# Up and gate products of a gated MLP by Strassen's scheme over even and odd tokens

## The chip, the core and the metric

The kernel runs on one core of one Trainium2 chip. The metric is the device time of one execution in microseconds (us), the median of the runs shown. A separate profiled execution gives the trace; its time is given beside the runs.

## The reference, cut to what matters

One decoder block over 1024 tokens with 16 meta tokens ahead of them, all in float32. The mixer (short convolution and stick-breaking attention) comes first; its output projection, a norm and a residual follow; then the gated MLP, which is the part that the change rewrites:

```python
D_MODEL, SEQ, N_META, CONV_WIDTH, D_FF = 1024, 1024, 16, 3, 2816

def conv_gated_mlp(xn, w_up_gate, conv_w_ffn, w_down):
    u, g = jnp.split(xn @ w_up_gate, 2, axis=-1)     # each (tokens, 2816)
    u = causal_dwconv(u, conv_w_ffn)                 # 3 taps per channel, along tokens
    return (jax.nn.gelu(u) * g) @ w_down

h = h + rms_norm(mix, g_post_mix)
h = h + rms_norm(conv_gated_mlp(rms_norm(h, g_pre_ffn), ...), g_post_ffn)
return h[:, N_META:, :]
```

## The kernel before

Every float32 product is made of three matmuls: an operand is split into a rounded part `hi` (a cast on ACT) and the remainder `lo` (a subtraction on POOL or DVE, in `split`), and hi x hi, hi x lo and lo x hi are added up in PSUM. 1026 tokens count for the MLP (1024 and two before them for the convolution), in three chunks of 342 or nine blocks of 114.

The stage before the MLP is the out-projection: for each of nine token blocks, `out_chunk` makes three PSUM chunks (24 matmuls each), and `post_block` does the first norm, the residual, and the second norm on DVE and ACT, ending in the row `xv`. A block's transposes (`transposed`, on PE) are emitted one block later; before, they write the MLP's input `xn2` straight from PSUM as hi and lo.

The MLP has 22 channel blocks of 128 for u and 22 for the gate. Each is an item of the class `Dense`: 512 KB of weights come in one DMA on the SP queue, are split once, and three chunks of 24 matmuls (8 feature blocks x 3) follow. A step of the outer loop (`NG` = 11) makes two u items and two gate items. Copies of u go to SBUF on ACT; `conv3` and the gelu run on ACT and DVE; a gate chunk is multiplied from PSUM on DVE, and the product is split into `ahi` and `alo`, the stationary operands of the down product. Down weights are split on POOL. A step's down product (`down`: 8 token blocks x 2 halves, 512 columns) is handed out between the dense chunks of the next step; the last step takes four channel blocks at once, and a norm, the residual and the output DMA follow per token block.

Engines take their instructions in order; a scheduler in the build orders them per engine from the written program and its dependencies. Tiles of a pool share buffers, and the first writer of a new tile waits for the last user of the old one.

Of the kernel before, what the change touches and what calls it, by code (L numbers as in the profile page):

```python
# [26 lines left out]
EPS = 1e-6  # L27


@with_exitstack  # L30
def block_kernel(ctx, tc, x, meta_tokens, g_pre_mix, w_in, channels, w_proj_conv,
# [28 lines left out]
    mm_d = tc.dram_tile([7, P, KB * QB], F32, name="mm_d")  # L60
    h_d = tc.dram_tile([NQ, D], F32, name="h_d")
# [94 lines left out]
    def col_block(w, c):  # L156
        return w[c]
# [407 lines left out]
    xnt_ctx.close()  # L565
    slots_de = ctx.enter_context(ExitStack())
# [3 lines left out]
    m_ctx = ctx.enter_context(ExitStack())  # L570
    mpool = m_ctx.enter_context(pool("mblk", 2))
# [54 lines left out]
    xn2 = []  # L626
    CHU = [(0, CH), (CH, CH), (2 * CH, CH)]
    CHG = [(2, CH - 2), (CH, CH), (2 * CH, CH)]
# [27 lines left out]
    s_ctx.close()  # L656
    psA.close()
# [6 lines left out]

    o_ctx = ctx.enter_context(ExitStack())
    ow = o_ctx.enter_context(pool("ow", 1, "right"))
    osml = o_ctx.enter_context(pool("osml", 4, "right"))
    g_post = ow.tile([P, D], F32, name="g_post")
    g_pre2 = ow.tile([P, D], F32, name="g_pre2")
# [3 lines left out]
    xn2 = [slot_tile(pl, "xn2") for pl in (slotD, slotE, slotF)]  # L673

    ff_items, act, conv_in = [], {}, {}
    dense3 = Dense(ps_mm2, ff_items)
# [3 lines left out]
    def load_m(b):  # L680
        if b in mb or b > 8:
            return
        raw = mpool.tile([P, KB, QB], F32, name="mraw", tag="mraw")
        nc.sync.dma_start(raw, mm_d[b - 2].rearrange("p (k n) -> p k n", k=KB))
        t = m_tile(b)
        split(t[:, 0], t[:, 1], raw)

    def out_chunk(b, c, ssq):
# [10 lines left out]
        sq = ow.tile([P, CH], F32, name="sq", tag="sq")  # L699
        nc.scalar.activation(sq[:QB, :n], ps, AF.Square, accum_out=ssq[:QB, c:c + 1])  # L700
        nc.vector.tensor_tensor(rows[b][:QB, cs], ps, g_post[:QB, cs], op=ALU.mult)

    def post_block(b, ssq):
        t = b * QB
        h = rows[b][:QB]
        xv = ow.tile([P, D], F32, name="xv", tag="xv", bufs=2)[:QB]
# [15 lines left out]
        def transposed():  # L722
            c, o = b // 3, (b % 3) * QB
            to_features(xn2[c][:, 0, :, o:o + QB], xn2[c][:, 1, :, o:o + QB], xv, QB, ps_tp2)
# [3 lines left out]
    ffn = {}  # L728

    def item_u(fb):  # L730
        def evac(ci, a, n, ps):
            if ci == 0:
                if fb == 0:
                    wk = slotC.tile([P, 2, KB, CH], F32, name="owork", tag="t")
                    ffn["wk"] = wk.rearrange("p a k n -> p (a k n)")
                conv_in[fb] = (ffn["wk"][:, fb * NQ:(fb + 1) * NQ] if fb < 2 else
                               ffn["u"].tile([P, NQ], F32, name="u", tag="u"))
            u = conv_in[fb]
            nc.scalar.copy(u[:, a:a + n], ps)
            if ci == 2:  # L740
                cv = ffn["u"].tile([P, D], F32, name="cv", tag="cv")
                conv3(cv, u, D, lambda k: w_ffn(k, fb))
                nc.scalar.activation(cv, cv, AF.Gelu_apprx_tanh)
                conv_in[fb] = cv
        return (col_block(w_up_gate, fb), src_of(xn2), CHU, evac)

    def item_g(fb):
        def evac(ci, a, n, ps):
            if ci == 0:
                act[fb] = (ffn["p"].tile([P, D], F32R, name="ahi", tag="ahi", bufs=4),  # L750
                           ffn["p"].tile([P, D], F32R, name="alo", tag="alo", bufs=4))
            ah, al = act[fb]
            c = slice(a - 2, a - 2 + n)
            cv = conv_in[fb][:, c]
            nc.vector.tensor_tensor(cv, cv, ps, op=ALU.mult)
            split(ah[:, c], al[:, c], cv)
        return (col_block(w_up_gate, NFF + fb), src_of(xn2), CHG, evac)

    NG = NFF // 2
    for gi in range(NG):  # L760
        ff_items += [item_u(2 * gi), item_u(2 * gi + 1), item_g(2 * gi), item_g(2 * gi + 1)]

    to_transpose = []
    for b in range(9):
        load_m(b + 1)
        rows[b] = ow.tile([P, D], F32, name="row", tag="row", bufs=2)
        sums = osml.tile([P, 3], F32, name="sums", tag="sums")
        for c in range(3):
            out_chunk(b, c, sums)
        if to_transpose:  # L770
            to_transpose.pop(0)()
        if b == 7:
            dense3.load(0)
            dense3.prep(0)
            dense3.load(1)
        post_block(b, sums)


    first = [dense3.run(0), dense3.run(1)]
    for g in (first[0], first[0], first[1], first[1]):  # L780
        for _ in range(8):
            next(g)
        if to_transpose:
            to_transpose.pop(0)()
    o_ctx.close()
    slots_abc.close()
    m_ctx.close()
    fu = ctx.enter_context(pool("fu", 2, "right"))
    fp = ctx.enter_context(pool("ffn", 2))
    fsml = ctx.enter_context(pool("fsml", 4))  # L790
    ffn["p"], ffn["u"] = fp, fu
    accs = [fp.tile([P, D], F32, name=f"acc{i}", bufs=1) for i in range(8)]

    def down_weights(fb, pl, tag, engine):
        raw = wpool.tile([P, D], F32, name="raw", tag="raw")
        nc.sync.dma_start(raw, w_down[fb * P:(fb + 1) * P, :])
        hi = pl.tile([P, D], F32R, name=tag + "hi", tag=tag + "hi")
        lo = pl.tile([P, D], F32R, name=tag + "lo", tag=tag + "lo")
        split(hi, lo, raw, engine)
        return hi, lo  # L800

    ssqs = {}

    def down(gi, wd):
        last = gi == NG - 2
        nj = len(wd)
        for tb in range(8):
            if last:
                ssqs[tb] = fsml.tile([P, 2], F32, name="fs", tag="fs")
            for hf in range(2):  # L810
                if last and hf:
                    ps = ps_mm2.tile([P, 512], F32, name="mm", tag="mm")
                else:
                    ps = ps_o.tile([P, 512], F32, name="po", tag="po")
                c = slice(hf * 512, (hf + 1) * 512)
                for j in range(nj):
                    ah, al = act[2 * gi + j]
                    hi, lo = wd[j]
                    th, tl = ah[:, tb * P:(tb + 1) * P], al[:, tb * P:(tb + 1) * P]
                    nc.tensor.matmul(ps, th, hi[:, c], start=(j == 0), stop=False)  # L820
                    nc.tensor.matmul(ps, tl, hi[:, c], start=False, stop=False)  # L821
                    nc.tensor.matmul(ps, th, lo[:, c], start=False, stop=(j == nj - 1))  # L822
# [5 lines left out]
                if last:  # L828
                    sq = fu.tile([P, NQ], F32, name="sq", tag="u")[:, :512]
# [3 lines left out]
            yield tb  # L833

    def ffn_steps(gi):
        if gi == 0:
            for g in first:
                for _ in range(9):
                    next(g, None)
                yield  # L840
            dense3.i = 2
        for _ in range(6 if gi == 0 else 12):
            dense3.chunk()
            yield

    pend, wd = None, []
    for gi in range(NG):
        for s, _ in enumerate(ffn_steps(gi)):
# [91 lines left out]
```

## Time and profile before

| | us |
|---|---|
| median of 3 runs | 2108.33 (2107.0 to 2110.51) |
| the profiled execution | 2109.53 |
| span of its trace, first to last instruction | 2107.8 |
| out-projection | 1245.70 to 1352.90 |
| MLP, to its last matmul | 1352.90 to 2095.97 |
| from there to the end | 11.83 |

The engines are PE (matmuls), PEld (its weight loads), DVE, ACT, POOL, and SP, which here only issues DMAs. Busy times come from the hardware profiler; the end of a matmul is modelled, so the duration shown is longer than the time that it takes in a stream, and the distance from one start to the next tells the latter. A mark such as [0.21 <-DVE xv L720] is idle time of the engine ahead of the instruction, and what ended it.

### The profile page before, as it was taken

The page shows a single profiled execution, that of the slowest core. Times are in us where ns is not written, and L with a number is a line of the kernel's source. Part 1 is how long each engine was busy: PE and PEld are TensorE (multiplying, and loading weights), DVE is VectorE, ACT ScalarE, POOL GpSimd, SP SyncE. Part 2 cuts the span into 40 slices and gives each one's busy share as a digit, 9 for nine tenths or more (in the row PEclk, how much of TensorE's full clock was granted, in tenths as well). Part 3 has the DMA queues.
Part 4 walks back from the last instruction along what each step waited for, and adds up shares of the span by engine and source line. Part 5 has one row for each costly group of instructions (what it writes and reads, how often), then busy time and mean ns, then how long its engine had stood idle before and what let it go on. Part 6 is the DMA issues. An engine that isn't in the chain of part 4 may idle for free.

```text
span 2107.8 us, 30776 instructions
## 1 busy us (share of the span) xinstructions
PE 2042.4 (97%) x12624; PEld 1958.1 (93%) x12624; DVE 1008.1 (48%) x1613; ACT 786.6 (37%) x1642; POOL 684.4 (32%) x591
## 2 busy tenths in 40 slices
PE   5999999999999999999999999999999999999997
PEld 5999999999999999999999999999999999999996
DVE  6455565655555555654331116543333343333436
ACT  4444454545454444544421124332222221222232
POOL 4443444444344434444122540032112221222123
PEclk9999999999999999999999999999999999999999
DMA  3111101111111111012584674221011110111124
GB/s 132 41 51 41 61 31 55 47 43 41 48 51 41 60 32 61 31 53 74 168 237 151 179 219 126 63 70 50 25 57 51 51 50 31 61 51 51 30 81 139
DMA packets 49689, 154.49 MB, mean 73 GB/s; under 512 B 12024, under 2 KB 12024, under 8 KB 49548
## 3 DMA queue, kind: packets, MB, share of 16 engines
q1 hardware_dynamic: 48396, 150.43, 22.7%
q8 instruction: 99, 1.62, 0.3%
q10 hardware_dynamic: 1152, 2.10, 0.3%
q14 instruction: 42, 0.34, 0.1%
HBM read 119.83 MB, written 32.68 MB: 72 GB/s over the span
## 4 chain that ended last, share of the span: by engine, by line
PE 86%; DVE 7%; ACT 3%; DMA 2%; issue 2%; POOL 1%; SPq 0%; DVEq 0%; ACTq 0%; POOLq 0%
PE mm L125 20%; PE mm L126 20%; PE mm L127 20%; PE po L820 3%; PE po L822 3%; PE po L821 3%; PE tp L369 3%; PE av L359 2%; PE av L360 2%; PE z L323 2%; PE z L322 2%; PE po L695 2%; PE po L697 2%; PE po L696 2%; DVE fl L333 1%
## 5 line engine op out<-in xcount | busy, mean ns | idle before, releaser
L66 POOL TENSOR_TENSOR wlo<-raw,whi 128x1024 fp32r<-128x1024 f32 x124 | 312.4, 2520 | 660.9 <-ACT whi L65 660.9
L125 PE MATMUL mm<-xnT,whi 128*128 128x342 f32 (+2 forms) x1536 | 508.3, 331 | 3.6 <-ACT xnT L65 3.6
L126 PE MATMUL mm<-xnT,whi 128*128 128x342 f32 (+2 forms) x1536 | 495.6, 323 | 0.5 <-DVE xnT L66 0.5
L127 PE MATMUL mm<-xnT,wlo 128*128 128x342 f32 (+2 forms) x1536 | 494.0, 322 | 0.0
L125 PE MATMUL mm<-xn,whi 128*128 128x342 f32 (+1 forms) x1056 | 337.8, 320 | 0.0
L126 PE MATMUL mm<-xn,whi 128*128 128x342 f32 (+1 forms) x1056 | 337.7, 320 | 0.0
L127 PE MATMUL mm<-xn,wlo 128*128 128x342 f32 (+1 forms) x1056 | 336.4, 319 | 0.0
L335 POOL TENSOR_TENSOR be<-be,fl 114x127 f32<-114x127 f32 (+2 forms) x144 | 176.9, 1228 | 404.0 <-DVE fl L333 193.2
L125 PEld LDWEIGHTS mm<-xnT,whi 128*128 128x128 f32 x1536 | 291.2, 190 | 8.3 <-ACT xnT L65 4.2
L126 PEld LDWEIGHTS mm<-xnT,whi 128*128 128x128 f32 x1536 | 292.0, 190 | 2.1 <-DVE xnT L66 1.0
L127 PEld LDWEIGHTS mm<-xnT,wlo 128*128 128x128 f32 x1536 | 291.2, 190 | 0.0
L65 ACT CAST whi<-raw 128x1024 fp32r<-128x1024 f32 x126 | 132.3, 1050 | 253.0 <-PE mm L126 221.2
L333 DVE TENSOR_TENSOR_SCAN fl<-fl 114x128 f32<-114x128 f32 (+2 forms) x144 | 204.9, 1423 | 4.9
L126 PEld LDWEIGHTS mm<-xn,whi 128*128 128x128 f32 x1056 | 199.7, 189 | 2.7
L125 PEld LDWEIGHTS mm<-xn,whi 128*128 128x128 f32 x1056 | 198.9, 188 | 2.8
L127 PEld LDWEIGHTS mm<-xn,wlo 128*128 128x128 f32 x1056 | 199.0, 188 | 0.0
L66 DVE TENSOR_TENSOR al<-tp,ah 128x342 fp32r<-128x342 f32 (+4 forms) x288 | 127.0, 450 | 139.5 <-ACT ah L65 137.5
L827 DVE TENSOR_TENSOR acc<-acc,po 128x512 f32<-128x512 f32 x136 | 93.1, 685 | 191.1 <-PE po L822 191.1
L65 ACT CAST ah<-tp 128x342 fp32r<-128x342 f32 (+4 forms) x288 | 112.9, 398 | 189.7 <-PE tp L369 181.8
L324 ACT ACTIVATE fl<-z 114x348 f32<-114x348 f32 (+10 forms) x240 | 111.4, 464 | 130.9 <-PE z L323 123.5
L369 PE MATMUL tp<-ident,be 114*128 114x114 f32 x720 | 119.6, 263 | 25.5 <-DVE al L66 20.9
L369 PEld LDWEIGHTS tp<-ident,be 114*128 114x128 f32 x720 | 89.1, 138 | 40.0 <-DVE al L66 29.7
(155 smaller groups left out, 3428.3 us busy)
## 6 DMA issues: line engine op xcount, KB each, us to landing
raw<-in_w_in_dram SPq DMA_DIRECT2D x64, 512.0 KB
raw<-in_w_up_gate_dram SPq DMA_DIRECT2D x44, 512.0 KB
raw<-in_w_down_dram SPq DMA_DIRECT2D x22, 512.0 KB
y_d<-yy SPq DMA_DIRECT2D x8, 513.0 KB
ga_d<-gt SPq DMA_DIRECT2D x8, 513.0 KB
o_d<-ot SPq DMA_DIRECT2D x8, 513.0 KB
gc_d<-gt SPq DMA_DIRECT2D x8, 513.0 KB
ld<-y_d SPq DMA_DIRECT2D x8, 513.0 KB
```

Of the source, the lines that this page charges most:

```text
L65: nc.scalar.copy(hi, src)
L66: (lo_engine or nc.vector).tensor_tensor(lo, src, hi.bitcast(F32), op=ALU.subtract)
L125: nc.tensor.matmul(ps, wh, xh, start=(kb == 0), stop=False)
L126: nc.tensor.matmul(ps, wh, xl, start=False, stop=False)
L127: nc.tensor.matmul(ps, wl, xh, start=False, stop=(kb == KB - 1))
L324: nc.scalar.activation(fl[:, c0:c0 + n], z, AF.Sigmoid, scale=-0.125)
L333: nc.vector.tensor_tensor_scan(fl[:, :nk][:, ::-1], fl[:, :nk][:, ::-1], fl[:, :nk][:, ::-1], 1.0, op0=ALU.mult, op1=ALU.min)
L335: nc.gpsimd.tensor_tensor(be[:, 0:nk - 1], be[:, 0:nk - 1], fl[:, 1:nk], op=ALU.mult)
L369: nc.tensor.transpose(tp[:n, QB * j:QB * (j + 1)], blocks[j][0][:, kb * P:kb * P + n], ident[:QB, :QB])
L820: nc.tensor.matmul(ps, th, hi[:, c], start=(j == 0), stop=False)
L821: nc.tensor.matmul(ps, tl, hi[:, c], start=False, stop=False)
L827: nc.vector.tensor_tensor(a, a, ps, op=ALU.add)
```

## The change

Up and gate products go by Strassen's scheme (Winograd's form), one level. The tokens are split into even (E) and odd (O), the 1024 features into two halves (1, 2), and two channel blocks of 128 make a pair; so each pair is a 2 x 2 by 2 x 2 product of blocks, with B11 = E1, B12 = O1, B21 = E2, B22 = O2 and weight quarters A11 to A22. Seven products of 12 matmuls take the place of eight. `x_early` and `x_late` make the seven token operands (B11, T1, T2, B21, T3, B22, T4) once, in two halves of 258 and 256 columns (`HALF`); `prep_pair` makes the seven weight operands of a pair with four sums on DVE, seven casts on ACT and seven subtractions on POOL, in a ring of eight tiles. A u pair runs two sets of products (258 and 256 columns), a gate pair one set of 512. `products` adds in PSUM: bank b1 is filled by A11 x B11, copied by ACT, and then gets S2 x T2 added, copied again, and so on. The out-projection's transposes now go to a float32 tile `xr`.

Down becomes a stage of its own: gated activations are stored to `act_d` in DRAM and loaded again, ten groups (nine of two channel blocks, one of four), with the same matmuls as before.

```diff
+HALF = [(0, 258), (258, 256)]
+NJ = 514
...
+    act_d = tc.dram_tile([DFF, D], F32, name="act_d")
...
-            to_features(xn2[c][:, 0, :, o:o + QB], xn2[c][:, 1, :, o:o + QB], xv, QB, ps_tp2)
...
+                        if j == 0:
+                            nc.scalar.copy(dst, src)
+                        else:
+                            nc.vector.tensor_copy(dst, src)
...
+    def x_early(c):
+        e1, o1 = quarter(c, "E1"), quarter(c, "O1")
+        op_split("B11", c, e1, nc.gpsimd)
+        sub(nc.vector, o1, o1, e1)
+        op_split("T1", c, o1, nc.vector)
+        sub(nc.vector, o1, quarter(c, "O2"), o1)
+        sub(nc.vector, e1, o1, e1)
+
+    def x_late(c):
+        op_split("T2", c, quarter(c, "O1"), nc.vector)
+        op_split("B21", c, quarter(c, "E2"), nc.gpsimd)
+        op_split("T3", c, quarter(c, "E1"), nc.vector)
+        sub(nc.vector, quarter(c, "E2"), quarter(c, "E2"), quarter(c, "O1"))
+        op_split("B22", c, quarter(c, "O2"), nc.gpsimd)
+        op_split("T4", c, quarter(c, "E2"), nc.vector)
...
+    def prep_pair(i):
...
+        keep("A11", a11)
+        nc.vector.tensor_tensor(tmp_s, a21, a22, op=ALU.add)
+        yield
+        keep("S1", tmp_s)
+        sub(nc.vector, a21, a11, a21)
+        sub(nc.vector, a11, tmp_s, a11)
+        yield
+        keep("S2", a11)
+        yield
+        keep("A12", a12)
+        sub(nc.vector, a12, a12, a11)
+        yield
+        keep("S3", a21)
+        yield
+        keep("S4", a12)
+        yield
+        keep("A22", a22)
+        load_pair(i + 1)
+        yield
...
+        b1, b3 = bank()[:, :n], bank()[:, :n]
+        mm(b1, "A11", "B11", True, True)
+        nc.scalar.copy(snap()[0][:, :n], b1)
+        yield
+        mm(b3, "S1", "T1", True, True)
+        nc.scalar.copy(snap()[1][:, :n], b3)
+        yield
+        mm(b1, "S2", "T2", False, True)
+        nc.scalar.copy(snap()[2][:, :n], b1)
+        yield
+        b2 = bank()[:, :n]
+        mm(b2, "A12", "B21", True, True)
+        evac(0, 0, b2, snap()[0][:, :n])
+        yield
+        mm(b1, "S3", "T3", False, True)
+        evac(1, 1, b1, snap()[1][:, :n])
+        yield
+        mm(b3, "S4", "B22", False, True)
+        evac(0, 1, b3, snap()[2][:, :n])
+        yield
+        mm(b1, "A22", "T4", False, True)
+        evac(1, 0, b1, None)
+        yield
...
+    def evac_g(p):
...
+            if s is None:
+                nc.vector.tensor_tensor(v, v, ps, op=ALU.mult)
+            else:
+                nc.vector.tensor_tensor(s, ps, s, op=ALU.add)
+                nc.gpsimd.tensor_tensor(v, v, s, op=ALU.mult)
...
+                nc.sync.dma_start(act_d[fb * P:(fb + 1) * P, :], cv)
...
+    for i in range(1, len(pairs)):
+        p, gate = divmod(i, 2)
+        if gate:
+            conv_gelu(p)
+            sets = [products(i, 1, 512, bank, evac_g(p))]
+        else:
+            sets = [products(i, j0, n, bank, evac_u(j0, n)) for j0, n in HALF]
...
+    groups = [[2 * g, 2 * g + 1] for g in range(9)] + [[18, 19, 20, 21]]
```

Two places where the order on an engine moves. The first is PE at the end of the out-projection: `po` is its last chunk, `tp_14167` (before) and `tp_14150` (after) are the transposes of the next-to-last token block, and `tp_14241` and `tp_14311` those of the last one, read from its `xv`. Before:

```order
L697 MATMUL po_14139<-w_o_12209,mb_13943 114x340
L175 MATMUL tp_14167<-ident_61,xv_14054 128x114 x4
L175 MATMUL tp_14174<-ident_61,xv_14054 128x114 x4
L125 MATMUL mm_14214<-xn2_13032,whi_14048 128x342
...
L126 MATMUL mm_14287<-xn2_13032,whi_14208 128x342
L175 MATMUL tp_14241<-ident_61,xv_14181 128x114 x4
L175 MATMUL tp_14248<-ident_61,xv_14181 128x114 x4
L127 MATMUL mm_14287<-xn2_13032,wlo_14209 128x342
```

After:

```order
L706 MATMUL po_14119<-w_o_12210,mb_13925 114x340
L735 MATMUL tp_14150<-ident_61,xv1_13048 128x114 x4
L735 MATMUL tp_14156<-ident_61,xv1_13048 128x114 x4
L844 MATMUL st_14215<-opB11_13038,a_op_14014 128x258
...
L848 MATMUL st_14216<-opT1_13039,a_op_14084 128x258
L735 MATMUL tp_14311<-ident_61,xv0_13047 128x114 x4
L735 MATMUL tp_14317<-ident_61,xv0_13047 128x114
L844 MATMUL st_14215<-opT2_14199,a_op_14116 128x258
```

Between the transposes of the last two blocks there stood 50 matmuls of 342 columns; now there stand 24 of 258, the first two products of the first pair.

The second is ACT from the end of a u pair to its gate pair. In the rows before, `u` are copies from PSUM, the ACTIVATE rows of `cv` the convolution's first tap and the gelu, `whi` the cast of a coming weight. Before:

```order
L65 CAST whi_15750<-raw_15632 128x1024
L739 COPY u_15659<-mm_15703 128x342
L193 ACTIVATE cv_15729<-u_15659,par_66 128x1024
L743 ACTIVATE cv_15729<-cv_15729 128x1024
L739 COPY u_15781<-mm_15756 128x342
```

After, with `a_op` a weight operand of the ring, `snap` the copy of a bank, `owork` the tile that holds u and cv:

```order
L68 CAST a_op_14740<-raw_14615 128x512
L859 COPY snap_14229<-st_14725 128x256
L68 CAST a_op_14770<-raw_14617 128x512
L68 CAST a_op_14800<-raw_14615 128x512
L68 CAST a_op_14829<-raw_14617 128x512
L196 ACTIVATE owork_14276<-owork_14276,par_66 128x1024
L897 COPY owork_14276<-st_14725 128x255
L196 ACTIVATE owork_14276<-owork_14276,par_66 128x1024
L68 CAST a_op_14859<-raw_14832 128x512
L853 COPY snap_14229<-st_14844 128x512
L976 ACTIVATE owork_14276<-owork_14276 128x1024
```

Where one cast of a whole weight stood, casts of half width stand between the bank copies, and the cast of the pair after next (`a_op_14859`, from the raw tile `raw_14832`) stands ahead of the gate pair's first bank copy (`st_14844`).

## Rows read from the trace of the kernel before

**Rows 1.** The page, part 1: engine, busy us (share of the span), instructions.

```profile
PE 2042.4 (97%) x12624; PEld 1958.1 (93%) x12624; DVE 1008.1 (48%) x1613; ACT 786.6 (37%) x1642; POOL 684.4 (32%) x591
```

**Rows 2.** Busy us (instructions): PE, PEld, DVE, ACT, POOL; granted clock, DMA share, GB/s.

```profile
1352.90:2095.97 743.07, 742.86 (x4241) 696.84 (x4239) 303.90 (x405) 187.77 (x287) 167.36 (x76) 1.00 0.17 56
2095.97:2107.80 11.83, 0.00 (x1) 0.00 (x0) 6.93 (x16) 1.65 (x5) 1.83 (x2) 0.62 0.24 89
```

**Rows 3.** Timeline of PE: start us, us, engine, line, operation; down, then gate.

```profile
1500.96 0.39 PE L820 MATMUL po<-dhi,ahi 128*128 128x512 f32 x1
...
1503.73 0.32 PE L125 MATMUL mm<-xn,whi 128*128 128x340 f32 x1
...
1505.92 0.32 PE L127 MATMUL mm<-xn,wlo 128*128 128x340 f32 x1
```

**Rows 4.** The page, part 5: operation, count, busy us, mean ns, idle.

```profile
L125 PE MATMUL mm<-xn,whi 128*128 128x342 f32 (+1 forms) x1056 | 337.8, 320 | 0.0
```

**Rows 5.** Timeline of PE: the two narrow kinds with full streams around them.

```profile
609.75 0.27 PE L359 MATMUL av<-ah,vv 128*128 128x228 f32 x1
609.86 0.27 PE L360 MATMUL av<-al,vv 128*128 128x228 f32 x1
609.97 0.33 PE L125 MATMUL mm<-xnT,whi 128*128 128x342 f32 x1
...
962.21 0.30 PE L322 MATMUL z<-kk,qh 128*114 128x292 f32 x1
962.34 0.29 PE L323 MATMUL z<-kk,ql 128*114 128x292 f32 x1
962.47 0.32 PE L125 MATMUL mm<-xnT,whi 128*128 128x342 f32 x1
```

**Rows 6.** Groups by line: casts and subtractions.

```profile
L66 POOL TENSOR_TENSOR wlo<-raw,whi 128x1024 fp32r<-128x1024 f32 x124 | 312.4, 2520 | 660.9 <-ACT whi L65 660.9
L65 ACT CAST whi<-raw 128x1024 fp32r<-128x1024 f32 x126 | 132.3, 1050 | 253.0 <-PE mm L126 221.2 <-DMA raw<-in_w_up_gate_dram 13.9 <-PE mm L127 6.2
L66 DVE TENSOR_TENSOR wlo<-raw,whi 128x1024 fp32r<-128x1024 f32 x2 | 2.5, 1226 | 0.9 <-ACT whi L65 0.9
L65 ACT CAST ahi<-cv 128x342 fp32r<-128x342 f32 (+1 forms) x66 | 31.2, 473 | 156.9 <-DVE cv L755 153.8 <-issue 3.0
```

**Rows 7.** Timelines of PE and ACT: a chunk's last matmul and its copy.

```profile
1369.67 0.31 PE L127 MATMUL mm<-xn,wlo 128*128 128x342 f32 x1
1370.03 0.45 ACT L739 COPY owork<-mm 128x342 f32<-128x342 f32 x1 [3.30 <-PE mm L127]
```

**Rows 8.** Timelines of SP and ACT: a weight load issued, its user.

```profile
1526.24 2.71 SPq L101 DMA_DIRECT2D raw<-in_w_up_gate_dram  x2
1529.90 1.05 ACT L65 CAST whi<-raw 128x1024 fp32r<-128x1024 f32 x1 [1.48 <-DMA raw<-in_w_up_gate_dram]
```

**Rows 9.** Timeline of PE: last matmul of the out-projection, transposes of the last block.

```profile
1352.67 0.33 PE L697 MATMUL po<-w_o,mb 128*114 128x340 f32 x1
...
1361.82 0.97 PE L175 MATMUL tp<-ident,xv 114*128 114x114 f32 x8 [0.21 <-DVE xv L720]
```

**Rows 10.** The columns of rows 2, around an idle stretch of PE.

```profile
968.00:972.00 4.00, 1.38 (x11) 1.10 (x10) 3.96 (x5) 0.95 (x3) 3.24 (x4) 1.00 0.51 130
972.00:976.00 4.00, 4.00 (x18) 4.00 (x18) 0.88 (x3) 0.69 (x2) 1.35 (x3) 0.57 0.00 0
976.00:980.00 4.00, 4.00 (x26) 3.91 (x25) 1.29 (x2) 2.29 (x6) 0.00 (x0) 1.00 0.00 0
```

**Rows 11.** Timelines of DVE and POOL where they work at the same time.

```profile
1378.60 3.30 POOL L66 TENSOR_TENSOR wlo<-raw,whi 128x1024 fp32r<-128x1024 f32 x1 [1.37 <-ACT whi L65]
1380.09 2.89 DVE L194 SCALAR_TENSOR_TENSOR cv<-owork,par,cv 128x1024 f32<-128x1024 f32 x1 [0.46 <-ACT cv L193]
1383.01 1.28 DVE L195 SCALAR_TENSOR_TENSOR cv<-owork,par,cv 128x1024 f32<-128x1024 f32 x1
```

**Rows 12.** The page, part 5: weight loads of up and gate.

```profile
L125 PEld LDWEIGHTS mm<-xn,whi 128*128 128x128 f32 x1056 | 198.9, 188 | 2.8
```

More of the change, by code (lines that the diff above doesn't have):

```diff
@@ L656, in block_kernel @@
     s_ctx.close()
+    slots_de.close()
     psA.close()
@@ L763, in block_kernel @@
     to_transpose = []
+    prep0 = prep_pair(0)
     for b in range(9):
         load_m(b + 1)
-        rows[b] = ow.tile([P, D], F32, name="row", tag="row", bufs=2)
+        rows[b] = rws[b % 2]
         sums = osml.tile([P, 3], F32, name="sums", tag="sums")
@@ L802, in block_kernel, with bank_of @@
[L802 to L806, printed above, removed]
+    ring_pool["ap"] = ctx.enter_context(pool("ap", 2, "right"))
+    late_ctx = ctx.enter_context(ExitStack())
+    late = late_ctx.enter_context(pool("late", 1, "right"))
+    for name in ("T2", "B21", "T3", "B22", "T4"):
+        ops[name] = late.tile([P, 2, 4, NJ], F32R, name=f"op{name}")
+    x_late(0)
+    def bank_of(pl, tag):
+        return lambda: pl.tile([P, 512], F32, name="st", tag=tag)
+    first = products(0, *HALF[0], bank_of(ps_mm2, "mm"), evac_u(*HALF[0]))
@@ new lines, in block_kernel @@
+    for k, _ in enumerate(first):
+        if k >= 1:
+            next(prep0, None)
+        if k == 5:
+            to_transpose.pop(0)()
+            x_early(1)
+            x_late(1)
+    for _ in prep0:
+        pass
+    prep = prep_pair(1)
+    for k, _ in enumerate(products(0, *HALF[1], bank_of(ps_o, "po"), evac_u(*HALF[1]))):
+        if k % 2:
+            next(prep, None)
+    psB.close()
+    psC = ctx.enter_context(ExitStack())
+    ps_st = psC.enter_context(pool("ps_st", 8, space=PSUM))
@@ new lines, in block_kernel @@
+    last_pair = len(pairs) - 1
+    for i in range(1, len(pairs)):
[3 more added lines that the diff above has]
+            sets = [products(i, 1, 512, bank, evac_g(p))]
+        else:
+            sets = [products(i, j0, n, bank, evac_u(j0, n)) for j0, n in HALF]
+        for _ in prep:
+            pass
+        prep = prep_pair(i + 1) if i < last_pair else prep_down_first()
+        for si, st in enumerate(sets):
+            for k, _ in enumerate(st):
+                if gate or (7 * si + k) % 2:
+                    next(prep, None)
@@ L807, in down @@
+    for gi, fbs in enumerate(groups):
+        last = gi == len(groups) - 1
+        for _ in prep:
+            pass
+        prep = iter(()) if last else prep_down(groups[gi + 1])
+        if gi == len(groups) - 2:
+            nc.sync.dma_start(g_post2, g_post_ffn.partition_broadcast(P))
+        if last:
+            for tb in range(2):
+                load_h(tb)
         for tb in range(8):
@@ L871, in block_kernel @@
[L871 to L882 removed]
+            next(prep, None)
```

318 lines of the change are left out of this document (192 added, 126 removed).

## Prediction

> **What bounds the kernel now.** I read the busy time first: TensorE (PE) works 97% of the span [rows 1]. Then the span in stages, the last one cut out: from the end of the out-projection (1352.90 us) to the last matmul PE is busy 742.86 of 743.07 us at a granted clock of 1.00, and 11.83 us of tail follow [rows 2]. DVE, ACT and POOL are busy 304, 188 and 167 us of those 743. So the change touches a stretch in which only matmuls set the time: whatever it takes from them is gained until another engine makes PE wait, and nothing hides such a wait.
>
> What a matmul costs is read from start to start, since the duration shown overlaps the next one. Twelve of 512 columns take 2.77 us, 0.231 each; fourteen of 340 take 2.19 us, 0.156 each [rows 3]. The stretch agrees: up and gate have 3 x 1056 = 3168 matmuls [rows 4], down has 22 x 16 x 3 = 1056 of 512 columns, 243.9 us; with about 1.2 us for the transposes of the last blocks, (743.07 - 243.9 - 1.2) / 3168 = 0.1572 us.
>
> **The products.** For each pair of channel blocks the old kernel issues 144 matmuls of 340 or 342 columns. The new one issues 84 per set: two sets (258 and 256 columns) for u, one of 512 for the gate. With 11 pairs of each kind that is 1848 narrow and 924 wide matmuls, 2772 in place of 3168. The wide ones cost 924 x 0.231 = 213.4 us. The trace has none of 258 columns. The nearest rows are 228 columns, with a full 128-column weight load, at 0.11 us, and 292 columns at 0.13 us [rows 5]; the line between them gives 0.119. I take 0.120 and keep 0.110 and 0.130 for the range: 1848 x 0.120 = 221.8 us (203 to 240). Before: 3168 x 0.1572 = 498.0. **Gain 62.8 us.** Down keeps its 1056 matmuls.
>
> By the Trainium skill, TensorE: Matmul & The Clock Gate, section Back-to-back issue gap, a warm matmul of N columns takes N/2.4 + 2.5 ns: 110 ns for 258 columns, and the sum would be 18 us lower. The trace differs: for 340 columns the rule gives 144 ns and the rows 156, so the rows stand.
>
> **Preparing the weights.** Per pair the old kernel made two casts (ACT, 1.05 us) and two subtractions (POOL, 2.52) of 1024 columns; the new one makes seven of 512 columns of each, plus four DVE sums. Half-width prices, between the shorter and the full rows [rows 6]: ACT 0.62, POOL 1.26, DVE 0.61 us. POOL gets 8.8 us per pair, 12.6 in a gate pair with three multiplications, ACT 4.3, DVE 2.5, against 20.2 us of PE for a u pair and 19.4 for a gate pair. In sum all fit; what counts is the order. The ring has eight operand tiles and a pair uses seven, so each new operand waits for the product one place earlier to finish, and six of the seven are made while the second set of u runs, one per product of 12 x 0.120 = 1.44 us. ACT is then in series with PE: the third product adds into the bank of the first, so it waits for the copy of that bank, and the order shows the operand's cast ahead of that copy. The hop from a product's last slot to ACT is 0.36 us after that matmul's start, 0.20 after its slot [rows 7]; 0.20 + 0.62 + 0.45 (the copy there, of 342 columns) = 1.27 us, against 1.44. It fits by 0.2.
>
> At the change from u to gate, ACT holds the cast of the pair after next ahead of the first bank copy. Its raw tile is freed by the S4 subtraction on POOL: not before 5 x 1.44 = 7.2 us into the second set, plus 0.20, 0.62 and 1.26, so 9.3, or 10.3 behind one busy DVE instruction. A 512 KB load took 3.66 us from issue to its user [rows 8]: it lands 2.9 to 3.9 us into the gate pair (the set ends at 10.1). Cast and copy bring it to 4.1 to 5.1; PE's third product is due at 2 x 2.77 = 5.5. Margin 0.4 to 1.4 us. In the other direction the gate pair's products are twice as long and nothing is close; its two stores of activations stand on SP's queue ahead of loads that wait for POOL longer than they do.
>
> With margins this thin I charge the 22 pairs 0.3 us each: **6 us**; ends 0 and 1.26 (one POOL instruction per pair, 28 us).
>
> **The start of the stage.** The last token block's row must pass norm, residual and second norm before its transposes: in the old kernel these started 9.0 us after the out-projection (1361.82 against 1352.67 and 0.16 for its last matmul), and PE filled that with 50 dense matmuls, waiting 0.21 us [rows 9]. The new order has 24 narrow matmuls there: 2.9 us and 0.75 of transposes, so PE stands still for about 5.3 us. What is late next is DVE: from 9.0 us on it stands in line with twelve operand instructions of 1.23 us, a copy and three evacuations (some 2 us), so the last operand of the second half is ready at 25.8; its 12 matmuls and about eight before them end at some 28. The pair's own PE work would have ended at 21.1. **Loss 7.** After an idle stretch the clock falls: 2.62 us of idle [rows 10] were followed by 4 us at a granted clock of 0.57, mostly the 1.2 GHz level, with 18 matmuls in place of 26, some 1.6 us. Part of that lies inside waits here: **1 us**. Ends: 5 and 12 for both.
>
> **The down stage.** Activations go to DRAM and come back (22 stores, 22 loads of 512 KB). SP issues them with DMA engines at a 0.17 share [rows 2], and a group's prep (4 x 2.52 = 10.1 us of POOL) lies under the 22.2 us of the group before. Not covered is the first group: its last operand reuses the tile that the last product reads, so POOL's 2.52 us start when PE is done; five matmuls (1.15 us) go first. **Loss 2** (0 to 4). Evacuation into the accumulators and the tail are the same instructions as before: 11.83 us.
>
> **Sum.** -62.8 + 6 + 8 + 2 = -46.8 us. The profiled execution took 2109.53 us, 1.2 above the median of three; 2062.7 there, 2061.5 against the median: I say 2062.
>
> **Rivals.** (a) *Contention of DVE and POOL.* An instruction of one shape took DVE 2.89 us while POOL worked and 1.28 alone, and POOL's took 3.30 [rows 11] against its mean of 2.52 [rows 6]. The new stage gives both more to do at once, and PE's seventh product waits for a DVE addition that stands behind a subtraction. If each of the 33 sets lost one POOL instruction (1.26 us) in place of 0.3 per pair, 42 - 6 = 36 us go: 2098. For it: margins of 0.2 us. Against: POOL's own work fills 44 to 65% of a pair. The Trainium skill, SBUF — State Buffer, section Who interferes with whom, says that a DVE instruction with two SBUF inputs and a GpSimd one that reads SBUF block each other, the later waiting in full. By that rule each meeting costs up to 1.26 us; the trace agrees with 2.89 against 1.28.
>
> (b) *Slower: the weight load late on ACT.* The place is the cast ahead of the bank copy at each of ten u-to-gate changes. Beyond a landing some 4.7 us after issue every further microsecond stops PE, and once the stop is of the size of rows 10 the clock adds 1.6. Landing 8.2 us after issue gives 3.5 + 1.6 = 5.1 us x 10: 2062 + 51 = 2113. It decides the sign from about 8 us on. Against: DMA runs at 17% here and the load took 3.66.
>
> (c) *Slower: the weight load in PE is the bound.* A load shows 188 ns [rows 12]; if narrow matmuls could not start closer than that, u takes 347 us and the time is 2187. Against: 0.11 us from start to start with full loads [rows 5].
>
> (d) *Better.* Narrow matmuls at 0.110 and no losses in the steady pairs: 2062 - 18 - 6 = 2038.
>
> That the change does not do what it says is excluded by the order: 396 matmuls fewer, 1848 of them narrow.
>
> **Chances.** Forecast, 2047 to 2075: 0.62. (a), 2075 to 2105: 0.18. (b): 0.07. (c) 0.04. (d): 0.09. The range leaves out most of (d) and the far ends of (a), and all of (b) and (c): 2046 to 2097. A measurement of this kernel tells about 0.2% (4 us) from no change: faster by more 0.86, within 0.03, slower 0.11.
>
> **What would show it.** Right: starts 0.119 to 0.121 us apart in the u sets and 0.231 in the gate sets; PE idle for about 5 us once, before the last block's transposes, waiting for DVE's xv; a u-and-gate couple every 39.5 to 40.5 us; no clock below 1.00 between the first pair and the end. Wrong: PE waiting for ACT's copy or DVE's addition at every set (rival a), for ACT behind a weight DMA at each gate pair (b), or narrow starts 0.19 apart (c). A stall of down's groups waiting for reloaded activations would break the step on the down stage.

## The result and the profile after

The changed kernel takes **2090.1 us** in the median (2088.7 to 2091.8) against 2109.4 (2107.0 to 2112.0), a ratio of 0.9909 with a 95% interval of 0.9891 to 0.9926. Measured again beside other kernels it gave 0.9911 (0.9891 to 0.9931). It is faster, by 19 us or 0.9%, where 47 were forecast; 2090 lies inside the range of 2046 to 2097, near its slow end.

The page's first part of the changed kernel (engine, busy us, share, instructions), beside [rows 1]: PE has 396 matmuls and 54 us less, POOL 224 us more.

```profile
PE 1988.2 (95%) x12228; PEld 1858.4 (89%) x12228; DVE 1070.9 (51%) x1685; ACT 851.7 (41%) x1769; POOL 908.1 (44%) x765
```

The stages of the changed kernel, in the columns of [rows 2]: the out-projection, the first u and gate pair, the other twenty pairs, and down. The first stage is 6 us longer than that of the kernel before, which is the single line under it.

```profile
1243.60:1357.15 113.55, 109.22 (x708) 108.25 (x707) 73.91 (x157) 42.60 (x111) 16.29 (x12) 0.98 0.39 122
1357.15:1423.90 66.75, 48.65 (x270) 42.80 (x269) 47.50 (x49) 32.68 (x49) 37.12 (x20) 0.85 0.09 30
1423.90:1827.50 403.60, 399.51 (x2522) 358.92 (x2521) 178.60 (x216) 166.60 (x287) 228.53 (x168) 1.00 0.24 82
1827.50:2075.00 247.50, 241.64 (x1057) 197.59 (x1055) 129.41 (x209) 51.41 (x76) 114.63 (x55) 1.00 0.36 119
```

```profile
1245.30:1352.83 107.53, 107.17 (x706) 106.71 (x705) 62.68 (x155) 40.25 (x108) 4.16 (x3) 1.00 0.43 129
```

So PE is as full as forecast in the third line (399.5 of 403.6 us at full clock), and it stands still or runs slowly in the second: 18 us idle, and a granted clock of 0.85 on average.

The price of a narrow matmul is what [rows 5] had promised. In PE's timeline of the changed kernel (start us, duration, engine, line, operation) 48 of 258 columns take 5.75 us, 0.120 each, and 12 of 512 columns 2.78, 0.232 each, as in [rows 3]:

```profile
1425.25 0.28 PE L844 MATMUL st<-opT,a_op 128*128 128x258 f32 x1
...
1431.00 0.28 PE L844 MATMUL st<-opB,a_op 128*128 128x258 f32 x1
...
1444.61 0.39 PE L844 MATMUL st<-opB,a_op 128*128 128x512 f32 x1
...
1447.39 0.39 PE L844 MATMUL st<-opT,a_op 128*128 128x512 f32 x1
```

Where PE waits in the second stage (last column: idle us before, and what ended it); the first row answers to the transposes of [rows 9], which waited 0.21 us:

```profile
1367.11 1.19 PE L735 MATMUL tp<-ident,xv 114*128 114x114 f32 x5 [6.25 <-DVE xv L728]
1369.93 0.58 PE L844 MATMUL st<-opT,a_op 128*128 128x258 f32 x1 [1.64 <-ACT opT L68]
1380.38 0.39 PE L846 MATMUL st<-opB,a_op 128*128 128x256 f32 x1 [0.98 <-POOL opB L69]
1385.82 0.56 PE L844 MATMUL st<-opT,a_op 128*128 128x258 f32 x1 [4.81 <-DVE owork L899]
1396.06 0.38 PE L844 MATMUL st<-opT,a_op 128*128 128x256 f32 x1 [0.57 <-ACT snap L859]
1401.17 0.38 PE L844 MATMUL st<-opT,a_op 128*128 128x256 f32 x1 [2.46 <-DVE owork L899]
```

Behind these waits stand two things. ACT's first cast for the late operands (T2, T3, T4, B21 and B22, made in `x_late`) waited 3.95 us for a store of the out-projection. Then DVE and POOL worked off the operands one after the other: from 1369.9 to 1396.4 us DVE's twelve instructions of 1.23 us and POOL's five of 2.52 lasted up to 2.8 times as long wherever both had work. The timelines of ACT, POOL and DVE (a row with x2 or x5 covers several instructions):

```profile
1368.77 1.11 ACT L68 CAST opT<-xr 128x1032 fp32r<-128x1032 f32 x1 [3.95 <-DMA h_d<-row]
1371.09 15.96 POOL L69 TENSOR_TENSOR opB<-xr,opB 128x1032 fp32r<-128x1032 f32 x5 [16.76 <-PE tp L735]
1369.91 1.24 DVE L69 TENSOR_TENSOR opT<-xr,opT 128x1032 fp32r<-128x1032 f32 x1 [2.95 <-ACT opT L68]
1372.06 2.57 DVE L69 TENSOR_TENSOR opT<-xr,opT 128x1032 fp32r<-128x1032 f32 x1 [0.31 <-ACT opT L68]
1374.56 6.86 DVE L763 TENSOR_TENSOR xr<-xr 128x1032 f32<-128x1032 f32 x2
1381.34 3.44 DVE L69 TENSOR_TENSOR opT<-xr,opT 128x1032 fp32r<-128x1032 f32 x1
```

Of the six microseconds that the out-projection loses, 4.5 stand at one place, in both traces of the changed kernel: PE waits 2.76 us for the row `xv` of block 5 (blocks are counted from 0 here), and its clock then falls. The other 1.4 are a wait near the start of the stage that the second trace does not have. PE's row at that place, and the stretch behind it in the columns of [rows 2]:

```profile
1331.80 1.52 PE L735 MATMUL tp<-ident,xv 114*128 114x114 f32 x8 [2.76 <-DVE xv L728]
```

```profile
1331.80:1338.00 6.20, 6.20 (x33) 6.20 (x34) 3.93 (x10) 1.58 (x4) 2.15 (x1) 0.72 0.24 77
```

The row is late because the early operands of the first half (B11, T1 and three subtractions, `x_early`) are made in the midst of block 5's norm: from its last PSUM chunk to its `xv` the norm takes 14.5 us on DVE instead of 8.8, and the 72 matmuls of the next block cover only 11.3. Two things stretch it: DVE's four instructions for these operands, some 1.2 us each, stand between its steps, and POOL holds up the steps themselves. While POOL makes the remainder of B11, a DVE instruction of the norm on 114 x 1 numbers takes 2.25 us, and another 1.01; the same steps in the kernel before (last row) took 0.22 and 0.16. The rows are POOL's, DVE's, and DVE's of the kernel before:

```profile
1319.61 3.30 POOL L69 TENSOR_TENSOR opB<-xr,opB 128x1032 fp32r<-128x1032 f32 x1 [67.73 <-ACT opB L68]
1320.68 2.25 DVE L79 SCALAR_TENSOR_TENSOR t<-s,v 114x1 f32<-114x1 f32 x1
1323.15 1.01 DVE L81 TENSOR_TENSOR s<-s,t 114x1 f32<-114x1 f32 x1
1328.85 1.22 DVE L763 TENSOR_TENSOR xr<-xr 128x1032 f32<-128x1032 f32 x1
1330.37 1.28 DVE L728 SCALAR_TENSOR_TENSOR xv<-row,s,g_pre 114x1024 f32<-114x1024 f32 x1
```

```profile
1320.67 0.22 DVE L76 SCALAR_TENSOR_TENSOR t<-s,v 114x1 f32<-114x1 f32 x1
```

### The profile page after: what moved, and what is told of

Read it like the earlier page. It is cut to its first block, busy times and chain, and to the rows that moved or that the text cites. A ratio compares the mean times of both kernels' runs of the same rounds, so it can differ in the third digit from the quotient of the medians.

```text
span 2086.9 us, 30864 instructions
## 1 busy us (share of the span) xinstructions
PE 1988.2 (95%) x12228; PEld 1858.4 (89%) x12228; DVE 1070.9 (51%) x1685; ACT 851.7 (41%) x1769; POOL 908.1 (44%) x765
## 5 line engine op out<-in xcount | busy, mean ns | idle before, releaser
L69 POOL TENSOR_TENSOR wlo<-raw,whi 128x1024 fp32r<-128x1024 f32 x80 | 205.7, 2572 | 189.9 <-ACT whi L68 189.9
L69 POOL TENSOR_TENSOR a_op<-raw,a_op 128x512 fp32r<-128x512 f32 (+1 forms) x134 | 185.7, 1400 | 96.7 <-ACT a_op L68 94.2
L844 PE MATMUL st<-opT,a_op 128*128 128x258 f32 (+2 forms) x528 | 172.3, 326 | 15.0 <-DVE owork L899 7.9
L846 PE MATMUL st<-opT,a_op 128*128 128x258 f32 (+2 forms) x528 | 169.7, 321 | 0.0
L848 PE MATMUL st<-opT,a_op 128*128 128x258 f32 (+2 forms) x528 | 169.6, 321 | 0.0
L68 ACT CAST a_op<-raw 128x512 fp32r<-128x512 f32 (+1 forms) x134 | 82.9, 628 | 161.5 <-DMA raw<-in_w_up_gate_dram 58.0
L1089 DVE TENSOR_TENSOR acc<-acc,st 128x512 f32<-128x512 f32 x144 | 98.4, 687 | 96.1 <-PE st L1084 96.1
L846 PE MATMUL st<-opB,a_op 128*128 128x512 f32 (+2 forms) x396 | 127.6, 322 | 1.0 <-POOL opB L69 1.0
L844 PE MATMUL st<-opB,a_op 128*128 128x512 f32 (+2 forms) x396 | 127.4, 322 | 0.0
L848 PE MATMUL st<-opB,a_op 128*128 128x512 f32 (+2 forms) x396 | 127.3, 321 | 0.0
```

The costliest lines, as they stand in the source:

```text
L68: nc.scalar.copy(hi, src)
L69: (lo_engine or nc.vector).tensor_tensor(lo, src, hi.bitcast(F32), op=ALU.subtract)
L844: nc.tensor.matmul(ps, wt[:, 0, k], xh, start=start and kb == 0, stop=False, skip_group_check=True)
L846: nc.tensor.matmul(ps, wt[:, 0, k], xl, start=False, stop=False, skip_group_check=True)
L848: nc.tensor.matmul(ps, wt[:, 1, k], xh, start=False, stop=stop and kb == 3, skip_group_check=True)
```

## The experiments

Theory after the first reading: the missing time sits at the start of the MLP, in the wait for the store and in the line of DVE and POOL. Rivals: the half clock that follows PE's idle time; the place of the early operands in DVE's queue; a loss in the steady pairs.

Medians differ by some us for a reason that no edit touches: from the start to the first matmul of the out-projection the traces take 1243.6 to 1256.2 us, and the two traces of the changed kernel alone 1243.6 and 1253.2. So the stages are compared, as lengths between the starts of matmuls in each trace, one trace per kernel (us): the out-projection from its first to its last; from there to the second u pair, in which PE's own work is 40.5 (transposes 0.9, 168 x 0.120, 84 x 0.231); the twenty other pairs; down.

| kernel | median, ratio (95%) | out-proj. | to second u pair | 20 pairs | down |
|---|---|---|---|---|---|
| before | 2109 to 2111 | 107.3 | | | |
| changed | 2090.1, 0.9909 (0.9891 to 0.9926) | 113.2 | 66.9 | 403.7 | 247.0 |
| changed, again | 2093.9, 0.9911 (0.9891 to 0.9931) | 111.4 | 67.0 | 403.0 | 247.1 |
| own pools | 2084.8, 0.9881 (0.9854 to 0.9908) | 112.5 | 62.3 | 399.7 | 247.0 |
| remainders on DVE | 2084.1, 0.9883 (0.9857 to 0.9910) | 108.2 | 63.4 | 403.5 | 248.7 |
| behind the norms | 2094.3, 0.9919 (0.9898 to 0.9941) | 107.5 | 68.6 | 402.9 | 247.0 |
| PE kept busy | 2089.7, 0.9906 (0.9883 to 0.9929) | 111.8 | 67.1 | 399.4 | 248.6 |
| no remainders | 2083.0, 0.9876 (0.9860 to 0.9893) | 111.6 | 60.3 | 402.3 | 248.6 |
| pools + DVE | 2080.7, 0.9863 (0.9844 to 0.9882) | 108.4 | 59.2 | 399.6 | 247.0 |
| all three | 2088.1, 0.9905 (0.9890 to 0.9920) | 107.0 | 63.9 | 401.3 | 247.0 |
| + weights on DVE | 2083.8, 0.9860 (0.9838 to 0.9882) | 108.1 | 52.3 | 408.2 | 247.1 |
| + copies on DVE | 2093.8, 0.9924 (0.9910 to 0.9939) | 108.2 | 61.2 | 408.4 | 248.6 |

### The changed kernel again

> The changed kernel once more, beside the others. The terms read from its first trace should come again if they are the kernel's and not the run's: out-projection 113 us, 67 us from its last matmul to the second u pair, 399 to 404 us from there to the down stage, 247 us of down stage; the part ahead of the out-projection may differ by some us.

The terms came again within 0.6 us, the out-projection within 1.8, of which 1.7 stand in its first two blocks, where only the first trace has the wait of 1.40 us.

### Own pools

```diff
-    late = late_ctx.enter_context(pool("late", 1, "right"))
     for name in ("T2", "B21", "T3", "B22", "T4"):
+        late = late_ctx.enter_context(pool(f"late{name}", 1, "right"))
```

> Each of the five late operands gets a pool of its own, so that only the one that lies over the out-projection's rows (T4) waits for the last row's store; the cast of T2 then waits for the last out-projection matmul alone. Theory (the missing time is the start of the stage: the wait for the store, and 24 matmuls of cover where 60 were possible): the cast of T2 starts within 1 us of the out-projection's end instead of 11.7 us after it, the first u set takes 18 to 21 us instead of 29.9, the second 12 to 15, and the kernel 2080 us (2077 to 2084). Rival (what counts is only the line of operand instructions on DVE and POOL, which starts behind the last norm in any case): no more than 3 us, 2087. Rival (the loss sits in the steady pairs or in the down stage): 2090.

In one pool the first late operand waited for what had lain anywhere under the pool, the last row's store included; with pools of their own only T4's cast still waits for that store, 0.55 us (third row). T2's cast starts 2.9 us before the out-projection's last matmul, and 60 matmuls of products stand ahead of the transposes instead of 24. But the stretch became 4.6 us shorter, not 10 or more. DVE, and then ACT and PE, of this kernel:

```profile
1355.93 1.22 DVE L69 TENSOR_TENSOR opT<-xr,opT 128x1032 fp32r<-128x1032 f32 x1
1369.29 1.28 DVE L728 SCALAR_TENSOR_TENSOR xv<-row,s,g_pre 114x1024 f32<-114x1024 f32 x1
1372.37 1.14 ACT L68 CAST opT<-xr 128x1032 fp32r<-128x1032 f32 x1 [0.55 <-DMA h_d<-row]
1370.72 1.75 PE L735 MATMUL tp<-ident,xv 114*128 114x114 f32 x8 [4.28 <-DVE xv L728]
```

The operand instructions now stand in DVE's queue ahead of the last block's norm, so the transposes come 13.9 us after the out-projection's last matmul (1370.72 - 1356.81) instead of 10.2, and everything of the second half with them. Theory and rival each had half: the wait was real, and what it had covered was DVE's line.

### Remainders on DVE

```diff
-        op_split("B11", c, e1, nc.gpsimd)
+        op_split("B11", c, e1, nc.vector)
```

(and so for B21 and B22)

> The remainders of B11, B21 and B22 are made on DVE instead of POOL, nothing else. Theory (DVE and POOL block each other there, so their 12 x 1.23 and 5 x 2.52 us add up to 27.4 us, as the trace shows from 1369.9 to 1396.4): 17 x 1.23 = 20.9 us on DVE alone, the second u set ends 5 to 6 us earlier, the kernel takes 2084.5 us (2082 to 2087). Rival (the two engines run side by side and DVE's own line of 14.8 us sets the end): DVE's line grows by 6.1 us and the kernel becomes slower, 2092 to 2096.

The stretch is 3.5 us shorter and, unforeseen, the out-projection 5.1, or 3.3 against the second trace of the changed kernel. Its norm of block 5 is hardly shorter, 13.9 us instead of 14.5, since B11's remainder now takes its turn on DVE. But the scheduler placed that block's transposes behind ten matmuls of the block after next instead of three, so that PE waited 1.13 us instead of 2.76, and the clock stayed at 1.00 (columns of [rows 2]):

```profile
1253.60:1361.90 108.30, 107.17 (x706) 106.52 (x705) 72.48 (x155) 42.40 (x109) 11.62 (x8) 1.00 0.40 128
```

In the stretch the theory holds. With five more instructions DVE's line is shorter (1374.8 to 1399.3, 24.5 us instead of 26.5), and each takes its 1.23 us as long as POOL is idle, from DVE's timeline:

```profile
1375.97 1.23 DVE L69 TENSOR_TENSOR opB<-xr,opB 128x1032 fp32r<-128x1032 f32 x1
1377.11 1.23 DVE L69 TENSOR_TENSOR opT<-xr,opT 128x1032 fp32r<-128x1032 f32 x1
1389.44 6.46 DVE L763 TENSOR_TENSOR xr<-xr 128x1024 f32<-128x1024 f32 x3
```

The last row, three instructions in 6.46 us, meets POOL at the weights of the next pair. The rival, that the engines run side by side, had the kernel slower; it became faster.

### Behind the norms

```diff
-            if b == 6 and c == 2:
-                x_early(0)
...
+        if b in (6, 7):
+            with tc.issue_after(xv_done.ins):
+                next(early0, None)
```

(with `x_early` cut into two steps that keep their order)

> The four DVE instructions of the early operands of the first half (two subtractions, one remainder, one subtraction) are queued behind the second norm of blocks 6 and 7, two behind each, instead of in between the norm of block 6. Theory (the out-projection takes 113.5 us instead of 107.5 because those instructions stand in front of block 6's norm, and PE's 2.8 us of waiting brings the half clock): the out-projection takes 107.5 to 109.5 us and the kernel 2085 us (2083 to 2088). Rival (the stage that follows starts from the last norm anyway and takes the gain back): 2088 to 2091.

The norm that matters is block 5's, not block 6's as expected above: `x_early` is written at block 6, and the scheduler set it among the steps of the norm before. Without DVE's four instructions that norm takes 11.25 us, though POOL's remainder of B11 still stands beside it (the same two steps take 1.71 and 1.02 us). The 72 matmuls of the next block (11.3 us) just cover that, and the out-projection is back at 107.5 us at full clock (the window of [rows 2]'s columns). The next stretch took 1.7 of the 5.7 back, in the first u set (31.8 us instead of 29.9, counted over its first 84 matmuls). The median of 2094.3 does not show the gain of 2 to 4 us that is left, and it lies above both theory and rival; the part ahead of the out-projection takes 1255.3 us in this trace.

```profile
1255.30:1363.00 107.70, 107.22 (x706) 106.55 (x705) 70.95 (x152) 42.14 (x109) 13.51 (x9) 1.00 0.42 128
```

### PE kept busy

```diff
+        if k == 1:
+            keep_busy(36)
```

> 36 matmuls of 258 columns into a PSUM bank that nobody reads are added behind the first two products, 4.3 us at full clock, where PE stands still for 6.2 us waiting for the last block's norm; all else is as it was. Theory (operands are late there, PE's clock is not what counts): the granted clock stays higher up to the transposes, but the sets end as before, 2089 to 2092. Rival (the loss is largely the half clock, 20 us of it in this stretch): 4 us or more are gained, 2086 or less.

The clock stayed at 1.00 up to the transposes, where the changed kernel's fell to 0.51 ahead of them (first fence this kernel, second the changed one, columns of [rows 2]), and nothing came of it: the sets took 30.1 and 15.1 us, as before.

```profile
1363.60:1374.60 11.00, 7.51 (x63) 7.12 (x61) 6.20 (x17) 2.89 (x7) 0.00 (x0) 1.00 0.14 42
1374.60:1381.40 6.80, 6.16 (x27) 5.80 (x28) 6.12 (x4) 5.36 (x7) 5.30 (x2) 0.50 0.00 0
```

```profile
1363.00:1376.60 13.60, 7.85 (x35) 7.25 (x36) 8.72 (x11) 7.54 (x10) 5.51 (x2) 0.51 0.11 34
```

That is as far as this run goes. The clock fell behind the transposes instead (the second row of the first fence), so 13.7 us of this stretch were at half clock instead of 20.5, and the part that went lay mostly over waiting. That half the clock costs nothing while the engine waits is shown; what the rest of it costs is not.

### No remainders in the second half

```diff
+        if c:
+            nc.scalar.copy(t[:, 0, :, j0:j0 + n], src)
+            return
```

> Left out: the seven remainders (lo) of the second half's token operands, four on DVE and three on POOL; the products of the second half read hi in their place, so the number and size of matmuls stay and the values are only rough. Theory (the line of operand instructions that DVE and POOL work off one at a time is what the first u pair waits for): 4 x 1.23 + 3 x 2.52 = 12.5 us of the 27.4 us go, and from the out-projection's last matmul to the second u pair it takes 54 to 57 us instead of 66.9; the whole some 11 us less than the changed kernel. Rival (POOL's share runs beside DVE's and costs nothing): 5 us or less. Rival (the end of the stretch is set by the norm and by ACT's casts): 2 us or less.

DVE's line shrank as the theory said, from 26.5 to 15.3 us (1376.4 to 1391.8). Only 6.7 of the 11 us reached the end, between theory and rival: the line was the bound for about seven of its microseconds. Then PE's own matmuls were, 68 in 15.4 us at a clock of 0.71 and 87 in 13.4 at 0.87, with 3.5 us of waiting for DVE's additions among them:

```profile
1373.60:1389.00 15.40, 11.78 (x68) 11.04 (x69) 12.05 (x10) 10.45 (x11) 5.86 (x2) 0.71 0.02 9
1389.00:1402.40 13.40, 11.83 (x87) 11.63 (x86) 5.57 (x7) 8.53 (x14) 6.11 (x5) 0.87 0.01 1
```

### Pools and remainders together, and all three

The edits above, combined.

> The pools of their own and the remainders on DVE together. If the two causes are separate (the late start of the line, and its length), the gains add up: out-projection 108 us, and 66.9 - 4.6 - 3.5 = 58.8 us from its last matmul to the second u pair; counted from the start of the out-projection 13 us less than the changed kernel. If they are one cause, 62 us and 9 us less.

59.2 and 108.4 us: the gains add up, 12.7 us from the start of the out-projection (10.9 against the second trace of the changed kernel, whose out-projection is 1.8 shorter). The two u sets now take 32.8 us instead of 45.0, but the first gate pair 25.5 instead of 21.1. PE waits 2 us each there for two of ACT's bank copies. The first stands on ACT behind convolution and gelu of u, those behind two casts of weights, and these waited for a DVE subtraction (last row) that had waited 3.00 us for POOL's weight remainders. POOL's first of those had lasted 7.05 us (first row), beside DVE's unbroken line (second and third row) and up to an instruction of DVE that reads PSUM (fourth):

```profile
1377.37 7.05 POOL L69 TENSOR_TENSOR a_op<-tmp_s,a_op 128x512 fp32r<-128x512 f32 x1 [25.83 <-ACT a_op L68]
1378.64 1.22 DVE L763 TENSOR_TENSOR xr<-xr 128x1024 f32<-128x1024 f32 x1
1382.05 1.22 DVE L69 TENSOR_TENSOR opT<-xr,opT 128x1024 fp32r<-128x1024 f32 x1
1383.18 0.42 DVE L899 TENSOR_TENSOR owork<-st,snap 128x255 f32<-128x255 f32 x1
1389.18 0.69 DVE L763 TENSOR_TENSOR raw<-raw 128x512 f32<-128x512 f32 x1 [3.00 <-POOL a_op L69]
```

> As before, and the early operands' DVE instructions queued behind the norms of blocks 6 and 7. With the remainders on DVE nothing of POOL stands in the way of block 6's norm any more, so little is left for this part: out-projection 107.5 to 108.2 us, and the operands that come later make the next stretch up to 2 us longer, as in the run of this part alone; 0 to 2 us more than without it. If it was the place of the DVE instructions that mattered, 1 us less.

The third part helped the out-projection by 1.3 us and cost the next stretch 4.7, more than expected. The early operands now stood between the out-projection's end and the last norm, and the transposes came 17.3 us after its last matmul instead of 12.4. Work moved out of one wait stayed in DVE's line.

### Weights of the first gate pair on DVE

```diff
-            split(t[:, 0], t[:, 1], src, nc.gpsimd)
+            split(t[:, 0], t[:, 1], src, nc.vector if i == 1 else nc.gpsimd)
```

> On top of own pools and remainders on DVE: the seven weight remainders of the first gate pair, too, are made on DVE instead of POOL. In the run before, POOL's first of them lasted 7.05 us instead of 1.26 while DVE worked without a break, and the first gate pair took 25.5 us instead of 19.4. Theory (DVE's unbroken line locks POOL out, and PE then waits for weights): the first gate pair takes 20 to 21.5 us, the second u set 1 to 2 us longer, and from the out-projection's last matmul to the second u pair it takes 55 to 57 us instead of 59.2. Rival (the weights are late because of ACT's casts): the first gate pair stays above 24.

The first gate pair takes 19.5 us, the second u set did not grow (12.7), and the stretch is down to **52.3 us** from 66.9 in the changed kernel, more than expected. The theory holds. But more than the 6.9 us gained here were given back later: the twenty pairs took 8.6 us longer, 5.5 at one place: the next u set's fifth product stood that long behind a bank copy, since ACT had to wait for the next pair's weights, whose two loads were issued one between and one behind the first two stores of activations (PE, then ACT):

```profile
1426.86 0.58 PE L844 MATMUL st<-opT,a_op 128*128 128x258 f32 x1 [5.47 <-ACT snap L859]
1425.91 0.62 ACT L68 CAST a_op<-raw 128x512 fp32r<-128x512 f32 x1 [6.94 <-DMA raw<-in_w_up_gate_dram]
```

### Bank copies on DVE

```diff
-        nc.scalar.copy(snap()[0][:, :n], b1)
+        nc.vector.tensor_copy(snap()[0][:, :n], b1)
```

(and so for the copy after the third product)

> On top of the last combination: the two copies of the bank that is added into (after the first and the third product of a set) go to DVE instead of ACT, where a cast that waits for the next pair's raw weights stands in front of them. Theory (what the steady pairs lose is this wait of PE for ACT behind a weight load, 0.3 to 2.2 us at each change from gate to u, and 5.8 us once in the last run): the first copy no longer stands behind the load, and from the second u pair to the down stage it takes 396 to 399 us instead of 399.5 to 408.2; the whole 2074 to 2078 us. Rival (DVE's sums wait for the same load and take ACT's place in front of the second copy, so that the wait moves by one product only): 400 to 406.

The theory fell and the rival held, with 408.4 us even beyond its 400 to 406. DVE's sums wait for the same load, the second copy stands behind them, and every u pair from the third on lost 0.9 to 1.2 us at its fifth product; the second u set grew as well, from 12.7 to 19.7 us, with the copies in DVE's line. The group of the products' first matmul, with what ended PE's idle time:

```profile
L844 PE MATMUL st<-opT,a_op 128*128 128x258 f32 (+2 forms) x528 | 172.4, 326 | 16.1 <-DVE snap L859 9.6 <-DVE snap L853 5.2 <-ACT a_op L68 0.7
```

The best median is that of own pools with the remainders on DVE: 2080.7 us, a ratio of 0.9863 whose interval lies wholly below the changed kernel's, 9 us better than that and 28 better than the kernel before. With the weights on DVE as well it is the same within the intervals. The intervals of own pools and of remainders on DVE alone overlap with the changed kernel's; that each of them gained is read from the stages.

## Why the prediction was wrong, term by term

**The products: right.** 0.120 and 0.231 us were taken, 0.120 and between 0.231 and 0.232 measured; u and gate come to 435.7 us of matmuls against 435.2. The 0.110 worked out from the Trainium skill's rule (TensorE: Matmul & The Clock Gate, section Back-to-back issue gap), which the section gives for an isolated matmul, is too low for this stream, as the rows of 340 columns had said.

**The steady pairs: right in size, wrong in place.** Twenty pairs take 403.7 us where their matmuls fill 396.1, a loss of 7.6 against 6.0 (3.3 to 7.6 in the traces where ACT makes the copies, but for the late load above). It is the wait of rival (b) at a tenth of its price, at the change from gate to u instead of u to gate. PE's waits in this stretch, then ACT's (us in total, times, longest):

```profile
PE st L844 <- ACT snap L853: 3.3, 3, 2.0
```

```profile
ACT a_op L68 <- DMA raw<-in_w_up_gate_dram: 52.4, 19, 6.0
```

ACT waits 52 us for weight loads, and only 3.3 reach PE as waits that the trace names. Read from start to start, 5.4 of the 7.6 stand at this place, the third product of the first u set, and the rest in gaps of some tenths.

**The down stage: a small miss, by luck.** 247.0 us against 243.9 + 2, but two errors nearly cancel. Its matmuls stand 0.227 apart, closer than taken: 239.7 us, 4.2 less. And it loses 7.3 us instead of 2, since PE waits for POOL not only at the first group but four more times at the last one, that of four channel blocks, from 2028 us on. PE's waits in this stage, in the same columns; the first group's 1.5 us is the last row:

```profile
PE st L1084 <- POOL dt L69: 2.7, 2, 1.4
PE st L1083 <- POOL dt L69: 1.5, 2, 1.1
PE st L1084 <- POOL a_op L69: 1.5, 1, 1.5
```

**The start of the stage: the step that failed.** 8 us were charged; the stretch to the second u pair takes 66.9 us for 40.5 of work, **a loss of 26.4**. Up to the last norm the walk was right within 1.3 us (transposes 10.2 us after the out-projection's last matmul, 6.25 us of idle PE in place of about 5.3), and it named the right engine as the next to be late. It then let DVE's line of twelve instructions begin 9.0 us after the out-projection's end and be done at 25.8; from that end (1357.0) it began at 12.9 and was done at 39.4.

- The start, 3.9 us, of which the norm is 1: the late operands share a pool whose ground reaches under the row that is being stored, so the first cast waits 3.95 us for that store, and DVE stands still for 2.95 of them. The prediction had no term for this; it did not ask what else had lain on that ground.
- The length, 26.5 us instead of 16.8: POOL's five remainders and DVE's twelve instructions take turns (12 x 1.23 + 5 x 2.52 = 27.4). [rows 11] had the price and rival (a) the mechanism, but it was spread over the steady pairs at 1.26 us a set, where 0.6 us of waiting for DVE's additions is all that the trace names, and left out of the one place in which both engines work without a break and PE has nothing else to do. So the time falls in the range given to (a), 2075 to 2105, but not on its path.
- Behind the line, 4 us more until the pair ends, 2.46 of them at full clock for a DVE addition (the last of PE's waits shown above), which stands behind a subtraction of weights that waits for POOL; and 1.7 in the first gate pair, 1.3 of them for a bank copy.

Taking the store and POOL out of it brings the stretch to 52.3 us, against the 49.1 that the forecast comes to (40.5 + 8 + 2 x 0.3): with these out of the way the walk is short by some 3 us. It did not describe this kernel.

**The out-projection: a term that was missing.** Nothing was charged to it; it is 5.9 us longer (4.1 in the second trace). The early operands of the first half were taken as free, beside a PE that is busy. But they stretch block 5's norm beyond the 11.3 us of matmuls that cover it, by DVE's four instructions and by POOL's one, which holds up the norm's short steps; 2.8 us of waiting and some 1.7 at half the clock are 4.5 of the loss. Moving DVE's four away is enough: then the stage takes 107.5 us, with POOL's one where it was. With that one on DVE it takes 108.2, mostly because the transposes are queued later.

In sum, against the forecast's span: 17.8 at the start of the stage (26.4 against 8.6 with the two pairs' share), 5.9 in the out-projection, 1.6 in the pairs, 1.1 in down (-4.2 and 5.3), 0.5 in matmuls, and -1.8 ahead of it all, which no edit touches: 25.1 of the 25.9 us by which the span of 2086.9 missed 2061.0.

## What to carry to other kernels

When matmuls are cut, look first at the start of the stage, where PE has the least to do: walk it engine by engine, with the two-input instructions of DVE and POOL in one line and not in two. Of a tile in memory that is used again, ask for the last reader and writer of everything under its pool, stores included. And before an instruction is put into a gap, look whose short steps are waiting in the same queue.

## What the runs showed of the hardware

DVE and POOL do not share by halves. A DVE instruction on 114 x 1 numbers in SBUF took 2.25 us instead of 0.22 while POOL's ran, and POOL's of 1.26 us took 7.05: it ended at 1384.42, just 1.24 us after DVE's unbroken row of 1.22 us instructions met one that reads PSUM (1383.18). So the one that waits may wait for a whole row of instructions, not for one. The Trainium skill, SBUF — State Buffer, section Who interferes with whom, calls the shared ports an exclusive lock and says that a DVE instruction with at most one input in SBUF, outside the two-port modes, does not contend with GpSimd. The trace agrees: three additions from PSUM took 1.09 us together in the midst of POOL's 15.96 us, and 1.08 with POOL idle.

Half the clock over a wait cost nothing. In the changed kernel's first pair it was granted for 13.7 and 6.8 us; with 36 unused matmuls ahead of the transposes it was granted for 6.8 and 6.8, and the sets took as long, since the engine was waiting for operands at either clock.
